# Feed-forward product order and later modulation copies in a one-core inference step

## The chip, the cores and the metric

The kernel runs on one core of a Trainium2 chip. The metric is the device time of one execution in microseconds, and three runs of the kernel before gave 1444.48, 1445.78 and 1446.87. TensorE (PE) multiplies, VectorE (DVE) and ScalarE (ACT) work on tiles, GpSimd (POOL) does some subtractions, and SyncE (SP) only issues DMAs; POOL and ACT can issue DMAs too. Every engine works through its own instructions in a fixed order, and semaphores make it wait for the others.

## The reference, cut to what matters

The reference is one layer of a backbone with two mixers for 128 context tokens and 512 latent tokens, in float32. The six modulation vectors come from a product with the large weight `ada_w`, the projection `w_in` has 10 x 1024 columns, and the feed-forward is a gated one with 2816 hidden columns:

```python
mod = (jax.nn.silu(cond) @ p['ada_w'] + p['ada_b']).reshape(cond.shape[0], N_MOD, D_MODEL)
h = x * (1.0 + scale1) + shift1
proj = h @ p['w_in']
...
x = layer_norm(ALPHA * x + gate1 * mix, p['ln1_g'], p['ln1_b'])
h = x * (1.0 + scale2) + shift2
gt, up = jnp.split(h @ p['ffn_w_in'], 2, axis=-1)
ff = (jax.nn.silu(gt) * up) @ p['ffn_w_out']
x = layer_norm(ALPHA * x + gate2 * ff, p['ln2_g'], p['ln2_b'])
```

## The kernel before

Each float32 matrix is split into a high part (`...h`) and the rest (`...l`), and a product is three passes on PE: high by high, low by high, high by low. The high part of a weight is a cast on ACT (line 619, through the helper `split`), the low part a subtraction on DVE (line 181, the helper through which all two-operand operations go, POOL's too).

Two stages multiply by a scheme in the manner of Winograd: seven products of half size instead of eight make two half blocks for two half token sets. The class `Wino` holds it. M1 (114 to 329 us) has 14 blocks of `w_in`, numbered 0 to 13, and its tiles begin with `m`; the feed-forward (1000 to 1282 us) has 22 blocks of `ffn_w_in`, and its tiles begin with `f`. A block j needs two raw weight tiles of 512 KB, row 0 and row 1 (`rm0_j`, `rm1_j` in M1, `rf0_j`, `rf1_j` in the feed-forward), out of a pool of three buffers. From these come the split tiles `g` (from row 0 as it is, products 1 and 2), `a` (product 4), and, after four subtractions on the raw tiles in place, `s` (product 6), `u` (5 and 7) and `v` (3). `gate` (token g) does the first, `rest` (token w) the others. A raw buffer is free for the next load once its last split is done: row 1 after `u`, row 0 after `v`. SP issues the loads in order.

Products 1, 6, 7 and 4 add up in one PSUM bank `a` (`ma`, `fa`), 2 in bank `b`, 5 and 3 in bank `c`. Between them the running sum is copied out by ACT (`keep`, line 676): `c1` after 1, `u2` after 6, `u3` after 7, of which product 4 must wait for the last since it adds to the same bank. DVE then adds the other banks to these copies, and product 5 of a block must wait until the `c` bank of two blocks earlier has been read by the addition into `u2`. In the profile's rows `u2` and `u3` are both `mu` or `fu`.

What sets the order: M1 follows PLAN, a string of tokens: `61` is product 6 of block 1, `g3` and `w3` are the weights of block 3, `Q9` is the modulation's product of quarter 9, i.e. half n = i mod 2 of modulation block nb = i div 2. The feed-forward follows PERIOD, one tuple of tokens with block offsets that is repeated for each j. Both give the order in which the program is written; a scheduler then orders every engine's instructions, and so a token that moves can also move ACT's and DVE's work. The modulation in M1: `ada_next` loads a quarter's weights of 1 MB (`araw`, one buffer, line 397), a Q step multiplies it (`ada_quad`, line 406), and after each second quarter `ada_vec` has ACT copy the sum out of PSUM into `md` (line 417); for blocks 4 and 5 and 10 and 11 PE then sums it over groups (`adag`, line 420), for the others it transposes it (`adaT`, line 430), DVE adds the bias, and the results go to `modT` or, by SP, to memory. `SY` in the code is SP, `G` is POOL.

Of the kernel before, what the change touches and what calls it, by code (L numbers as in the profile page):

```python
# [115 lines left out]
    return {k: np.ascontiguousarray(v) for k, v in c.items()}  # L116


PLAN = """x0 k0 L0 k1 x4 k2 p mlp t L1 T0 x3 T4 A0 x2 D0 T2 A1 x1 L2 B0 M0 T1 D2 A2 M2 T3 h0 L3 B1 D1 A3 h1 B2 M1 D3 h2 h3 M3 h4 W2 W0 h5 h6 h7 W1 q V0 e0 B3 g0 W3 V1 m w0 e2 10 20 g1 50 11 60 g2 70 21 30 40 w1 w2 61 51 52 12 71 Q8 62 22 g3 w3 13 41 g4 53 72 Q9 42 31 63 w4 g5 23 14 w5 73 Q10 43 32 g6 w6 64 24 15 54 74 Q11 33 65 25 44 16 26 55 75 Q12 g7 34 w7 66 45 56 17 76 Q13 35 67 46 g8 27 57 w8 18 77 Q14 g9 g10 36 w9 28 19 68 37 29 58 78 Q15 69 47 59 w10 79 Q16 38 110 210 g11 610 49 111 510 39 48 w11 211 g12 611 112 w12 212 710 Q17 g13 511 711 Q18 410 113 w13 311 612 310 411 512 712 Q19 513 213 613 412 713 312 413 313"""
HMOD = "SVSSVSSS"  # L120
HSUB = "GVVVVGVG"
WSUB = "VGGVVGGG"
# [6 lines left out]
FFNP = "1-1 2-1 g1 w1"  # L129
FFNT = ("g2", "", "")  # L130
FFN0 = "51 61 12 22 w2 71"
PERIOD = (("g", 1), ("w", 1), ("6", 0), ("4", -1), ("1", 1), ("5", 0), ("7", 0), ("3", -1), ("2", 1))
WPRI = 2
HIE = """SSSSVVSVSVSSSSSSSVVVSVVSVSSVSSSSSSSSSSSSSSSSSSSSSSSSSSSSSSSSSSSSSSSSSSSSSSSSSSSSSSSSSSSSSSSSSSSSSSSSSSSSSSSSSS"""
LOOK = """22222012202102201120122111222222222222222222222222222222222222222222222222222222222222222222222222222222222222"""
# [27 lines left out]
def body(tc, I, O):  # L163
    nc = tc.nc
    V, S, G, PE, SY = nc.vector, nc.scalar, nc.gpsimd, nc.tensor, nc.sync
# [14 lines left out]
    def tt(out, a, b, op, eng=None):  # L180
        return (eng or V).tensor_tensor(out=out, in0=a, in1=b, op=op)  # L181
# [7 lines left out]
    def pool(name, bufs=1, space=None, side=None):  # L189
        kw = dict(name=name, bufs=bufs, reuse_waits="tile")  # L190
        if space is not None:
            kw["space"] = space
        if side is not None:
            kw["side"] = side
        cm = tc.tile_pool(**kw)
        p = cm.__enter__()
        return p, (lambda: cm.__exit__(None, None, None))
# [19 lines left out]
    def mm_bank(nm):  # L217
        return bank("mm", nm)
# [20 lines left out]
    w1 = sp.tile([EMB, ORD], F32, name="w1")  # L239
# [12 lines left out]
    w2 = sp.tile([P, ORD], F32, name="w2")  # L252
    w3 = sp.tile([P, 2, ORD], F32, name="w3")
# [122 lines left out]
    def run_unit(u):  # L376
        n = len(u.specs)
        pos = stream["pos"]
        advance(pos, n)
        ws = stream["hl"][pos:pos + n]  # L380
        stream["pos"] = pos + n
        u.fn(*ws)
# [12 lines left out]
    def ada_load(nb, i, q, tag, bufs, eng=SY):  # L395
        raw = q.tile([P, 4, 512], F32, tag=tag, bufs=bufs, name=f"araw{nb}_{i}")
        eng.dma_start(raw, ada_w.rearrange("(k p) n -> p k n", p=P)[:, 4 * i:4 * i + 4, nb * 512:nb * 512 + 512])
        ada["raw"][nb, i] = raw

    def ada_quad(nb, i):  # L400
        raw = ada["raw"].pop((nb, i))
        if i == 0:
            ada["ps"][nb] = mm_bank(f"ada{nb}")
        ps = ada["ps"][nb]
        for g in range(4):
            PE.matmul(ps[32 * g:32 * g + 32, :], scT[:, 4 * i + g, :], raw[:, g, :], start=i == 0, stop=i == 1)

    def ada_mods(nb, q):
        with tc.high_priority():
            for i in range(2):  # L410
                ada_quad(nb, i)
            ada_vec(nb, q)

    def ada_vec(nb, q):
        part, half = nb // 2, nb % 2
        md = q.tile([P, 512], F32, tag="md", bufs=1, name=f"md{nb}")
        S.copy(md, ada["ps"].pop(nb))
        if part in (2, 5):
            p2 = mm_bank(f"adag{nb}")
            PE.matmul(p2[0:2, :], cst[:, 128:130], md, start=True, stop=True)  # L420
            gr = q.tile([2, 512], F32, tag="md", bufs=1, name=f"gr{nb}")
            SY.dma_start(gr, I["ada_b"][:, nb * 512:nb * 512 + 512].to_broadcast([2, 512]))
            tt(gr, p2[0:2, :], gr, ALU.add)
            V.tensor_scalar(gr, gr, 1.0 / ALPHA, None, ALU.mult)
            SY.dma_start(gd[part // 3, :, half * 512:half * 512 + 512], gr)
            return
        slot = {0: 0, 1: 1, 3: 2, 4: 3}[part]
        p2 = mm_bank(f"adaT{nb}")
        for i in range(4):
            PE.transpose(p2[:, i * P:i * P + P], md[:, i * P:i * P + P], ident)  # L430
        v = p2.rearrange("p (k g r) -> p k g r", k=4, g=4)[:, :, :, 0:2]
        dst = modT[:, slot, half * 4:half * 4 + 4, :]
        b0 = 17 + slot * 8 + half * 4
        tt(dst, v[:, :, 0], prT2[:, b0:b0 + 4].unsqueeze(2).to_broadcast([P, 4, 2]), ALU.add)
        for g in range(1, 4):
            tt(dst, v[:, :, g], dst, ALU.add)
# [3 lines left out]
    vp, close_vp = pool("vp")  # L440
# [7 lines left out]
    def x_load(t):  # L448
        xs = se.tile([P, D], F32, tag="xs", bufs=3, name=f"xs{t}")
        SY.dma_start(xs, x_tok[t])  # L450
        return xs

    def x_transpose(t, xs):
        for q in range(2):
            ps = sc_bank(f"xT{t}_{q}")
            for k in range(4):
                PE.transpose(ps[:, k * P:k * P + P], xs[:, (4 * q + k) * P:(4 * q + k + 1) * P], ident)
            for i in range(2):
                cpy("x", 2 * t + q, xT.tiles[2 * q + i][:, :, t * P:t * P + P],
                    ps[:, i * 256:i * 256 + 256].rearrange("p (k t) -> p k t", k=2))  # L460
# [51 lines left out]
    def ktab(i):  # L512
        cs = slice(i * 768, i * 768 + 768)
        raw = wp.tile([P, 768], F32, tag="raw", bufs=RAW_BUFS, name=f"kt{i}")
        SY.dma_start(raw, I["kt"][:, cs])
        cpy("k", i, kth[:, cs], raw)
        tt(ktl[:, cs], raw, f32(kth[:, cs]), ALU.subtract, G if KSUB[i] == "G" else V)

    def kern_load(cc):
        c0 = cc * 256  # L520
        w4 = se.tile([P, 2, 256], F32, tag="w4", bufs=2, name=f"w4_{cc}")
        for hf in range(2):
            SY.dma_start(w4[hf * ORD:hf * ORD + ORD],
                         I["filt_w4"][0].rearrange("o (a n) -> o a n", a=2)[:, :, c0:c0 + 256])
        win = sp.tile([P, NB, 256], F32, tag="win", bufs=2, name=f"win{cc}")
        SY.dma_start(win, I["win"][:, :, c0:c0 + 256])
        return w4, win, skp_all[:, c0:c0 + 256]
# [68 lines left out]
    def kern_store(cc, out):  # L596
        for t, f, n in out:
            KQ.dma_start(kd[cc, :, f:f + n], t)
# [24 lines left out]
    class Wino:  # L623
# [70 lines left out]
        def period(self, j, n):  # L694
            return self.run(" ".join(f"{t}{j + d}" for t, d in PERIOD if 0 <= j + d < n))

# [25 lines left out]
    def start():  # L722
        stream["stop"] = 4
        xs, ld, ab = {}, {}, {}

        def step(op, i):
            if op == "x":
                xs[i] = x_load(i)
            elif op == "T":
                x_transpose(i, xs[i])  # L730
            elif op == "L":
                ld[i] = kern_load(i)
            elif op == "A":
                ab[i] = kern_a(i, ld[i])
            elif op == "B":
                ab[i] = kern_b(i, ab[i])
            elif op == "W":
                kern_store(i, ab[i])
            elif op == "k":
                ktab(i)  # L740
            elif op == "D":
                for n in range(2):
                    ada_load(i, n, se, "araw", 3)
            elif op == "Q":
                nb, n = divmod(i, 2)
                ada_quad(nb, n)
                if i < M1_ADA[1] * 2 - 1:
                    ada_next(i + 1)
                if n == 1:
                    ada_vec(nb, mo["y"])  # L750
            elif op == "M":
                ada_mods(i, se)
            elif op == "h":
                make_h(i)
            elif op == "V":
                run_unit(vu[i])
            elif op == "e":
                m1_operands(i)
            elif op == "m":
                m1_open()  # L760
            elif op in "gw1234567":
                m1.run(op + str(i))()
            else:
                dict(p=params_load, t=params_T, q=params)[op]()

        for tok in PLAN.split():
            if tok == "mlp":
                if HP:
                    with tc.high_priority():
                        filter_mlp()  # L770
                else:
                    filter_mlp()
                continue
            step(tok[0], int(tok[1:] or 0))


    M1 = []
# [4 lines left out]
    mo = {}  # L782
# [78 lines left out]
    m1 = Wino("m", lambda tag: mo["p"], m1_x, m1_cols, m1_done, M1PRI)  # L861

    def ada_next(i):
        ada_load(*divmod(i, 2), vp, "v", 1, G)

    def m1_open():
        close_sp()
# [917 lines left out]
```

## Time and profile before

| | us |
|---|---|
| median of three runs | 1445.78 |
| profiled execution | 1444.85 |
| its span, first to last instruction | 1442.4 |
| PE busy | 1382.4 (96%) |
| DVE busy | 998.9 (69%) |
| ACT busy | 617.4 (43%) |
| POOL busy | 72.6 (5%) |

The profile is one execution. A timeline row gives the start, the duration, the engine, the line, the operation with its tiles, and, in square brackets, how long the engine sat idle before it and what ended that. The busy share of PE is an average: it is full in the middle of the run and has gaps in M1 and in the feed-forward. Where the clock is given it is the mean granted TensorE clock of a stretch, 1.00 being the upper of its two levels, 2.4 GHz, and 0.50 the lower, 1.2 GHz.

### The profile page before, as it was taken

The page shows a single profiled execution, that of the slowest core. Times are in us where ns is not written, and L with a number is a line of the kernel's source. Part 1 is how long each engine was busy: PE and PEld are TensorE (multiplying, and loading weights), DVE is VectorE, ACT ScalarE, POOL GpSimd, SP SyncE. Part 2 cuts the span into 40 slices and gives each one's busy share as a digit, 9 for nine tenths or more (in the row PEclk, how much of TensorE's full clock was granted, in tenths as well). Part 3 has the DMA queues.
Part 4 walks back from the last instruction along what each step waited for, and adds up shares of the span by engine and source line. Part 5 has one row for each costly group of instructions (what it writes and reads, how often), then busy time and mean ns, then how long its engine had stood idle before and what let it go on. Part 6 is the DMA issues. An engine that isn't in the chain of part 4 may idle for free. (4 is left out here: it accounts for less than half of the span.)

```text
span 1442.4 us, 23457 instructions
## 1 busy us (share of the span) xinstructions
PE 1382.4 (96%) x9513; PEld 1297.4 (90%) x9513; DVE 998.9 (69%) x1751; ACT 617.4 (43%) x1011; POOL 72.6 (5%) x68
## 2 busy tenths in 40 slices
PE   5999999989999999999999999999999999999997
PEld 2698888889999998999999999988999999998886
DVE  6886775745888853638888786568977667756427
ACT  3654544432333211446665655227644344542111
POOL 4320000011000000000000000000000000000003
PEclk9999999999999999999999999999999999999999
DMA  7934665557333364432232223551343333257211
GB/s 245 327 136 139 210 194 156 169 183 251 96 92 92 107 211 146 144 119 83 63 102 61 76 57 113 180 182 73 109 123 104 108 115 106 88 177 278 83 59 73
DMA packets 195783, 195.63 MB, mean 136 GB/s; under 512 B 7581, under 2 KB 155773, under 8 KB 194908
## 3 DMA queue, kind: packets, MB, share of 16 engines
q1 hardware_dynamic: 188524, 167.17, 37.1%
q0 software_dynamic: 5424, 21.73, 4.3%
q10 hardware_dynamic: 1728, 5.24, 0.9%
q8 instruction: 74, 1.21, 0.3%
q14 instruction: 33, 0.27, 0.1%
HBM read 162.91 MB, written 31.21 MB: 135 GB/s over the span
## 5 line engine op out<-in xcount | busy, mean ns | idle before, releaser
L181 DVE TENSOR_TENSOR wl<-raw,wh 128x1024 fp32r<-128x1024 f32 x96 | 117.3, 1224 | 133.4 <-ACT wh L357 132.4
L357 ACT CAST wh<-raw 128x1024 fp32r<-128x1024 f32 x90 | 94.1, 1049 | 221.2 <-PE pb L611 41.0
L1423 PE MATMUL fo<-wh,act 128*128 128x512 f32 (+1 forms) x440 | 130.7, 380 | 0.0
L1423 PEld LDWEIGHTS fo<-wh,act 128*128 128x128 f32 x440 | 81.3, 188 | 15.9
L1423 PE MATMUL fo<-wl,act 128*128 128x512 f32 (+1 forms) x220 | 83.4, 379 | 0.0
L611 PE MATMUL hy<-hTh,wh 128*128 128x320 f32 x256 | 79.6, 311 | 0.0
L611 PE MATMUL hy<-hTh,wl 128*128 128x320 f32 x256 | 79.2, 309 | 0.0
L611 PE MATMUL hy<-hTl,wh 128*128 128x320 f32 x256 | 79.2, 309 | 0.0
L611 PE MATMUL f<-hTh,wh 128*128 128x320 f32 x224 | 70.8, 316 | 0.0
L611 PE MATMUL f<-hTl,wh 128*128 128x320 f32 x224 | 69.7, 311 | 0.0
L611 PE MATMUL f<-hTh,wl 128*128 128x320 f32 x224 | 69.3, 309 | 0.0
L181 POOL TENSOR_TENSOR y<-y,gb 128x512 f32<-128x512 f32 x8 | 11.6, 1454 | 900.8 <-ACT y L170 900.5
L1423 PEld LDWEIGHTS fo<-wl,act 128*128 128x128 f32 x220 | 41.4, 188 | 7.9
L611 PEld LDWEIGHTS hy<-hTh,wh 128*128 128x128 f32 x256 | 48.1, 188 | 0.0
L611 PEld LDWEIGHTS hy<-hTl,wh 128*128 128x128 f32 x256 | 48.1, 188 | 0.0
L611 PEld LDWEIGHTS hy<-hTh,wl 128*128 128x128 f32 x256 | 48.1, 188 | 0.0
L170 ACT ACT_TABLE_LOAD x36 | 46.2, 1283 | 1.4 <-PEq L1769 0.7
L707 PE MATMUL v<-wl,hTh 128*128 128x256 f32 x160 | 44.9, 285 | 1.6 <-DVE wl L181 1.6
L707 PE MATMUL v<-wh,hTl 128*128 128x256 f32 x160 | 45.1, 285 | 0.2 <-POOL hTl L181 0.2
L707 PE MATMUL v<-wh,hTh 128*128 128x256 f32 x160 | 44.8, 285 | 0.0
L611 PEld LDWEIGHTS f<-hTl,wh 128*128 128x128 f32 x224 | 42.2, 188 | 0.0
L611 PEld LDWEIGHTS f<-hTh,wh 128*128 128x128 f32 x224 | 42.2, 188 | 0.0
(2291 smaller groups left out, 4730.9 us busy)
## 6 DMA issues: line engine op xcount, KB each, us to landing
raw<-in_w_in SPq DMA_DIRECT2D x52, 512.0 KB, 3.8
rf<-in_ffn_w_in SPq DMA_DIRECT2D x42, 512.0 KB, 4.0
araw<-in_ada_w POOLq DMA_DIRECT2D x16, 1024.0 KB, 5.7
rm<-in_w_in SPq DMA_DIRECT2D x28, 512.0 KB, 3.8
raw<-in_ffn_w_out SPq DMA_DIRECT2D x22, 512.0 KB, 3.7
sd<-my SPq DMA_DIRECT2D x28, 320.0 KB, 3.6
araw<-in_ada_w SPq DMA_DIRECT2D x8, 1024.0 KB, 11.3
kk<-kd SPq DMA_DIRECT2D x20, 256.0 KB, 3.1
```

Of the source, the lines that this page charges most:

```text
L170: r = S.activation(out, in_, func, bias=bias, scale=scale)
L181: return (eng or V).tensor_tensor(out=out, in0=a, in1=b, op=op)
L357: (V.tensor_copy if HIE[i] == "V" else S.copy)(hi, raw)
L611: r = PE.matmul(ps[:, 0:HT], w[a][:, k, :], x[b][:, k, c0:c0 + HT], start=k == 0 and i == 0, stop=k == kt - 1 and i == 2)
L707: PE.matmul(ps[:, (t - t0) * 256:(t - t0) * 256 + 256], hT[b][:, k, t * P:t * P + P], w[a][:, k % 4, :], start=k == 0 and i == 0, stop=k = ...
L1423: PE.matmul(ps, x(t, b, k0 + kk), w[a][:, kk, :], start=first and kk == 0 and i == 0, stop=last and kk == nk - 1 and i == 2)
```

## The change

Three things change. In PERIOD product 1 of the next block stands ahead of product 4 of the last. In PLAN `ada_vec` is no longer done by the second Q step of a modulation block but by tokens of its own, Z4 to Z9, each set some nine steps later: Z4 stands ahead of Q10 where the copy was part of Q9, Z5 behind Q12 where it was part of Q11, and the last, Z9, at the very end of PLAN. And `ada_next` no longer passes `G`, so the twelve `araw` loads of M1 are issued by SP.

```diff
-PERIOD = (("g", 1), ("w", 1), ("6", 0), ("4", -1), ("1", 1), ("5", 0), ("7", 0), ("3", -1), ("2", 1))
+PERIOD = (("g", 1), ("w", 1), ("6", 0), ("1", 1), ("4", -1), ("5", 0), ("7", 0), ("3", -1), ("2", 1))
...
                 if i < M1_ADA[1] * 2 - 1:
                     ada_next(i + 1)
-                if n == 1:
-                    ada_vec(nb, mo["y"])
+            elif op == "Z":
+                ada_vec(i, mo["y"])
...
     def ada_next(i):
-        ada_load(*divmod(i, 2), vp, "v", 1, G)
+        ada_load(*divmod(i, 2), vp, "v", 1)
```

In the feed-forward this is DVE's row around the weights of blocks 13 and 14, before (a name is the tile, its block and a number; `wfg14l` is the low part of the `g` tile of block 14):

```order
L181 TENSOR_TENSOR wfg14l_12101<-rf0_14_12098,wfg14h_12100 128x1024
L181 TENSOR_TENSOR rf1_13_11973<-rf0_13_11967,rf1_13_11973 128x512
L181 TENSOR_TENSOR rf0_13_11967<-rf1_13_11973,rf0_13_11967 128x512
L181 TENSOR_TENSOR rf0_13_11967<-rf0_13_11967 128x512
L181 TENSOR_TENSOR wfs13l_11983<-rf0_13_11967,wfs13h_11982 128x512
L181 TENSOR_TENSOR wfu13l_11987<-rf1_13_11973,wfu13h_11986 128x1024
L181 TENSOR_TENSOR fu3_11_11931<-fc11_11906,fu3_11_11931 128x320
L181 TENSOR_TENSOR wfv13l_11992<-rf0_13_11967,wfv13h_11991 128x512
L181 TENSOR_TENSOR fu2_10_11745<-fc10_11775,fu2_10_11745 128x320
```

And the same row in the changed kernel:

```order
L181 TENSOR_TENSOR wfg14l_12101<-rf0_14_12098,wfg14h_12100 128x1024
L181 TENSOR_TENSOR wfa13l_11976<-rf1_13_11973,wfa13h_11975 128x512
L181 TENSOR_TENSOR y10_11702<-fa10_11616,y10_11702 128x320
L181 TENSOR_TENSOR rf1_13_11973<-rf1_13_11973 128x512
L181 TENSOR_TENSOR rf1_13_11973<-rf0_13_11967,rf1_13_11973 128x512
L181 TENSOR_TENSOR rf0_13_11967<-rf1_13_11973,rf0_13_11967 128x512
L181 TENSOR_TENSOR rf0_13_11967<-rf0_13_11967 128x512
L181 TENSOR_TENSOR wfu13l_11987<-rf1_13_11973,wfu13h_11986 128x1024
L181 TENSOR_TENSOR wfs13l_11983<-rf0_13_11967,wfs13h_11982 128x512
L181 TENSOR_TENSOR wfv13l_11992<-rf0_13_11967,wfv13h_11991 128x512
L181 TENSOR_TENSOR fu3_11_11931<-fc11_11906,fu3_11_11931 128x320
L181 TENSOR_TENSOR fu2_10_11745<-fc10_11775,fu2_10_11745 128x320
```

The split `wfa13l` and the first subtraction on `rf1_13` stood ahead of `wfg14l` and now stand behind it, with a `y` product between them; `wfs` and `wfu` change places, and both `fu` additions come after `wfv13l`. ACT's casts move in the same way.

At M1's start this is ACT's row before:

```order
L619 CAST wmg2h_1442<-rm0_2_1440 128x1024
L676 COPY mc1_1_1424<-ma1_1411 128x320
L619 CAST wma1h_1510<-rm1_1_1508 128x512
L676 COPY mu2_0_1438<-ma0_1361 128x320
L619 CAST wmu1h_1521<-rm1_1_1508 128x1024
L676 COPY mu3_0_1458<-ma0_1361 128x320
```

And in the changed kernel:

```order
L619 CAST wmg2h_1442<-rm0_2_1440 128x1024
L676 COPY mc1_1_1424<-ma1_1411 128x320
L676 COPY mu2_0_1438<-ma0_1361 128x320
L676 COPY mu3_0_1458<-ma0_1361 128x320
L619 CAST wma1h_1510<-rm1_1_1508 128x512
```

Both copies of block 0's sums now stand ahead of the cast `wma1h`, which needs a loaded tile.

On SP, in the changed kernel, the loads around blocks 10 to 12 of M1 stand like this (`araw7_1` is the second quarter of modulation block 7, `sd` stores a finished half block):

```order
L397 DMA araw7_1_2475<-in_ada_w 128x4x512
L633 DMA rm1_10_2683<-in_w_in 128x8x128
L633 DMA rm0_11_2786<-in_w_in 128x8x128
L845 DMA sd_137<-my0_6_2151 128x640
L845 DMA sd_137<-my0_7_2389 128x640
L397 DMA araw8_0_2640<-in_ada_w 128x4x512
L845 DMA sd_137<-my1_7_2456 128x640
L397 DMA araw8_1_2727<-in_ada_w 128x4x512
L633 DMA rm1_11_2886<-in_w_in 128x8x128
```

The three `araw` rows stood on POOL before; the other rows of SP keep their order there.

## Rows read from the trace of the kernel before

**Rows 1.** The page's head: the span and the busy time of the engines.

```profile
span 1442.4 us, 23457 instructions
...
PE 1382.4 (96%) x9513; PEld 1297.4 (90%) x9513; DVE 998.9 (69%) x1751; ACT 617.4 (43%) x1011; POOL 72.6 (5%) x68
```

**Rows 2.** Stretches of the span: their length, then the busy time of each engine with its number of instructions, the granted clock, the DMA share and GB/s.

```profile
950.00:1000.00 50.00, 50.00 (x254) 42.40 (x253) 39.53 (x89) 24.33 (x44) 0.00 (x0) 1.00 0.29 95
...
1084.87:1227.96 143.09, 136.10 (x913) 133.38 (x912) 100.08 (x163) 61.12 (x109) 0.00 (x0) 1.00 0.36 107
```

**Rows 3.** What PE waited for from 100 to 360 us: total in us, times, the longest; the row on a weight tile.

```profile
PE ma L668 <- DVE wms11l L181: 0.5, 1, 0.5
```

**Rows 4.** The timeline of PE: the single instructions of M1 ahead of which it waited over 1 us.

```profile
127.71 0.41 PE L668 MATMUL ma<-m7h,wmu0h 128*128 128x320 f32 x1 [3.18 <-ACT mu L676]
...
165.27 0.42 PE L668 MATMUL mc<-m5h,wmu3h 128*128 128x320 f32 x1 [1.73 <-DVE mu L181]
...
190.09 0.59 PE L420 MATMUL adag<-md,cst 128*2 128x512 f32 x1 [1.05 <-ACT md L417]
...
220.26 0.33 PE L430 MATMUL adaT<-cst,md 128*128 128x128 f32 x1 [1.92 <-ACT md L417]
...
288.11 0.33 PE L430 MATMUL adaT<-cst,md 128*128 128x128 f32 x1 [1.64 <-ACT md L417]
...
307.01 0.63 PE L668 MATMUL mc<-m5h,wmu12h 128*128 128x320 f32 x1 [4.00 <-DVE mu L181]
```

**Rows 5.** The timeline of ACT from 126 us.

```profile
126.71 0.62 ACT L619 CAST wma1h<-rm 128x512 fp32r<-128x512 f32 x1 [3.14 <-DMA rm<-in_w_in]
127.24 0.42 ACT L676 COPY mu<-ma 128x320 f32<-128x320 f32 x1
```

**Rows 6.** The timelines of DVE and of POOL around 302 us, with an earlier row of DVE of the same form.

```profile
287.69 1.22 DVE L181 TENSOR_TENSOR wmu12l<-rm,wmu12h 128x1024 fp32r<-128x1024 f32 x1
...
302.58 3.37 DVE L181 TENSOR_TENSOR wmu13l<-rm,wmu13h 128x1024 fp32r<-128x1024 f32 x1
...
302.15 2.72 POOL L181 TENSOR_TENSOR wl<-raw,wh 128x1024 fp32r<-128x1024 f32 x1 [7.50 <-DVE wh L357]
```

**Rows 7.** Stretches that begin where a wait of PE ended, of PE alone: length, busy time with its number of instructions, granted clock, DMA share, GB/s.

```profile
127.71:134.00 6.29, 6.29 (x32) 0.73 0.01 3
220.26:226.00 5.74, 5.74 (x30) 0.70 1.00 324
307.01:315.00 7.99, 7.99 (x35) 0.61 0.91 290
1141.64:1144.00 2.36, 2.36 (x16) 1.00 0.08 22
...
288.11:292.00 3.89, 3.89 (x28) 1.00 0.98 338
```

**Rows 8.** Two lines of the page on DMA issues (KB each, median us from issue to landing), and the timelines of POOL, SP and ACT around 260 us.

```profile
araw<-in_ada_w POOLq DMA_DIRECT2D x16, 1024.0 KB, 5.7
rm<-in_w_in SPq DMA_DIRECT2D x28, 512.0 KB, 3.8
...
259.00 0.75 POOL L397 DMA_DIRECT2D araw<-in_ada_w  x1 [7.92 <-PE ada L406]
...
259.47 1.59 SPq L633 DMA_DIRECT2D rm<-in_w_in  x2
...
268.31 1.05 ACT L619 CAST wmg12h<-rm 128x1024 fp32r<-128x1024 f32 x1 [5.39 <-DMA rm<-in_w_in]
```

**Rows 9.** What PE waited for from 995 to 1285 us, and two rows of its timeline: the start of product 5 of block 12, and a wait ahead of product 4.

```profile
PE fa L668 <- ACT fu L676: 8.5, 12, 1.3
...
1155.28 0.42 PE L668 MATMUL fa<-t4h,wfa11h 128*128 128x320 f32 x1 [1.08 <-ACT fu L676]
...
1158.90 0.31 PE L668 MATMUL fc<-xxh,wfu12h 128*128 128x320 f32 x1
```

**Rows 10.** The chain that ended last, in order of time, its longest pieces: start, us, what.

```profile
1157.19 6.20 DMA rf<-in_ffn_w_in
1170.94 5.20 DMA rf<-in_ffn_w_in
...
1237.36 1.76 PE fc L668 x12
```

**Rows 11.** The timeline of ACT, two turns of the feed-forward's loop.

```profile
1149.66 1.05 ACT L619 CAST wfg14h<-rf 128x1024 fp32r<-128x1024 f32 x1 [2.41 <-DMA rf<-in_ffn_w_in]
...
1163.41 1.05 ACT L619 CAST wfg15h<-rf 128x1024 fp32r<-128x1024 f32 x1 [2.44 <-DMA rf<-in_ffn_w_in]
```

**Rows 12.** The timeline of DVE in the same turn.

```profile
1150.75 1.23 DVE L181 TENSOR_TENSOR wfg14l<-rf,wfg14h 128x1024 fp32r<-128x1024 f32 x1 [2.04 <-ACT wfg14h L619]
...
1154.94 1.23 DVE L181 TENSOR_TENSOR wfu13l<-rf,wfu13h 128x1024 fp32r<-128x1024 f32 x1 [0.25 <-ACT wfu13h L619]
...
1156.48 0.68 DVE L181 TENSOR_TENSOR wfv13l<-rf,wfv13h 128x512 fp32r<-128x512 f32 x1
...
1161.00 0.69 DVE L181 TENSOR_TENSOR wfa14l<-rf,wfa14h 128x512 fp32r<-128x512 f32 x1 [1.94 <-ACT wfa14h L619]
1161.73 0.69 DVE L181 TENSOR_TENSOR rf<-rf 128x512 f32<-128x512 f32 x1
```

**Rows 13.** The timeline of SP.

```profile
1156.19 1.75 SPq L633 DMA_DIRECT2D rf<-in_ffn_w_in  x2
```

More of the change, by code (lines that the diff above doesn't have):

```diff
@@ L116, in _constants @@
     return {k: np.ascontiguousarray(v) for k, v in c.items()}
-PLAN = """x0 k0 L0 k1 x4 k2 p mlp t L1 T0 x3 T4 A0 x2 D0 T2 A1 x1 L2 B0 M0 T1 D2 A2 M2 T3 h0 L3 B1 D1 A3 h1 B2 M1 D3 h2 h3 M3 h4 W2 W0 h5 h6 h7 W1 q V0 e0 B3 g0 W3 V1 m w0 e2 10 20 g1 50 11 60 g2 70 21 30 40 w1 w2 61 51 52 12 71 Q8 62 22 g3 w3 13 41 g4 53 72 Q9 42 31 63 w4 g5 23 14 w5 73 Q10 43 32 g6 w6 64 24 15 54 74 Q11 33 65 25 44 16 26 55 75 Q12 g7 34 w7 66 45 56 17 76 Q13 35 67 46 g8 27 57 w8 18 77 Q14 g9 g10 36 w9 28 19 68 37 29 58 78 Q15 69 47 59 w10 79 Q16 38 110 210 g11 610 49 111 510 39 48 w11 211 g12 611 112 w12 212 710 Q17 g13 511 711 Q18 410 113 w13 311 612 310 411 512 712 Q19 513 213 613 412 713 312 413 313"""
+PLAN = """x0 k0 L0 k1 x4 k2 p mlp t L1 T0 x3 T4 A0 x2 D0 T2 A1 x1 L2 B0 M0 T1 D2 A2 M2 T3 h0 L3 B1 D1 A3 h1 B2 M1 D3 h2 h3 M3 h4 W2 W0 h5 h6 h7 W1 q V0 e0 B3 g0 W3 V1 m w0 e2 10 20 g1 50 11 60 g2 70 21 30 40 w1 w2 61 51 52 12 71 Q8 62 22 g3 w3 13 41 g4 53 72 Q9 42 31 63 w4 g5 23 14 w5 73 Z4 Q10 43 32 g6 w6 64 24 15 54 74 Q11 33 65 25 44 16 26 55 75 Q12 Z5 g7 34 w7 66 45 56 17 76 Q13 35 67 46 g8 27 57 w8 18 77 Z6 Q14 g9 g10 36 w9 28 19 68 37 29 58 78 Q15 69 47 59 w10 79 Q16 38 110 210 Z7 g11 610 49 111 510 39 48 w11 211 g12 611 112 w12 212 710 Q17 g13 511 711 Q18 410 113 w13 311 612 Z8 310 411 512 712 Q19 513 213 613 412 713 312 413 313 Z9"""
 HMOD = "SVSSVSSS"
```

## The prediction

> **What bounds the kernel now.** I read the page's head first: TensorE (PE) is busy 1382.4 of 1442.4 us [rows 1], so only about 60 us of idle time and any time at a low clock can be won. Then I read PE's waits by stage. In the middle, from 350 to 1000 us, PE is nearly full (50.00 us busy in 950 to 1000 [rows 2]), and whatever the first Winograd stage ("M1", 114 to 329 us) wins or loses passes through it to the end. Two stages wait. In M1 PE waits for single copies on ScalarE (ACT) and subtractions on VectorE (DVE) [rows 4]. In the feed-forward it waits 8.5 us in all, 12 times, at most 1.3, for ACT's copy `fu` of the seventh product, always ahead of the fourth product [rows 9].
>
> What paces the feed-forward is another matter. The chain that ended last has no PE in its long pieces from 1003 to 1233 us: it goes from one `rf` weight load to the next [rows 10], and PE is busy 136.10 of 143.09 us [rows 2]. The loop in one block, with t = 0 at the gate cast `wfg14h` at 1149.66: DVE's `wfg14l` at 1.09, the raw-tile subtractions at 2.23 and 3.68, `wfu13l` at 5.28 to 6.51, `wfv13l` until 7.50 [rows 12]; the two issues of the next `rf` loads begin at 1156.19, t = 6.53 [rows 13]; the second of them, 6.20 us in the chain from 1157.19 [rows 10], ends the idle time of ACT and lets `wfg15h` start at 1163.41 [rows 11]. That is 13.75 us a turn, against PE's seven products of 1.76 us [rows 10], 12.3. So the stream of weights is the pace, and PE's wait for `fu` is how it is held to that pace: the copy stands in ACT's row behind the casts of a later block.
>
> **The change, part by part.** *Modulation copies (tokens Z).* Each `md` copy and what PE does with it moves some nine steps later; the copy then has many products of cover. PE's waits for `md` go: 1.05 + 1.92 + 1.64 = 4.61 us [rows 4]. The same transposes, additions and stores are issued later, none is saved or added.
>
> *What the scheduler reorders in M1.* The 3.18 us at 127.71 come from ACT: the copy `mu` (0.42 us at 127.24) stood behind `wma1h`, which waited 3.14 us for a DMA [rows 5]. In the changed order both `mu` copies stand ahead of `wma1h`, so PE's product 7(0) no longer waits; the cover is the products up to 5(1), which needs `wmu1l`, and by these rows that comes perhaps 0.4 us late. The 4.00 us at 307.01 come from DVE: `wmu13l` took 3.37 us, while `wmu12l` of the same form took 1.22, and GpSimd (POOL) ran `wl` from 302.15 to 304.87 [rows 6]. `mu` of block 11, for which PE waited, stood behind it. Now `wmu13l` and that `mu` stand ahead of the cast that starts POOL's `wl`, so this wait goes too. What is beside POOL's `wl` then is `wmv13l`, with `mu` of block 10 behind it, which PE's 5(13) needs: between 0 and 2.15 (3.37 - 1.22), I take 1.0, since PE comes there two products later.
>
> The GPSIMD Engine Reference of the Trainium skill (1. Specifications) says that GpSimd shares its way into SBUF with VectorE and that DVE instructions with two SBUF inputs contend with it. The long `wmu13l` agrees; by that rule `wmv13l` is stretched and the 1.0 would rather be 2.15, by a private port it would be 0.
>
> *The clock.* After three of these waits the granted clock was low for a while, means of 0.73, 0.70 and 0.61 over the 6.29, 5.74 and 7.99 us behind them, where 1.00 is the upper and 0.50 the lower of its two levels [rows 7]. Lost is (1 - clock) x length: 1.70 + 1.72 + 3.12 = 6.54 us, and this goes with the waits. After the wait of 1.64 at 288.11 and after one in the feed-forward it stayed at 1.00 [rows 7].
>
> *`araw` loads on SP's queue.* Twelve loads of 1 MB leave POOL's queue and stand in SP's, in order; ten of them directly or nearly ahead of a weight load `rm`. Each waits for PE to be done with the `araw` before it, and what stands behind it waits too. The trace of before has no such queue in M1. Lower bound 0: in before the same bytes share the same engines (5.7 us from POOL's queue, 3.8 for an `rm` [rows 8]). Upper bound: an `rm` lands half an `araw` later, 2.85 us, wherever PE has no slack. Such a place is near 277 us, where PE already waits for `wms11l` [rows 3] and ACT waited 5.39 us for the `rm` of `wmg12h` [rows 8]; three loads stand close to it (`araw7_1`, `araw8_1`, `araw9_0`): 8.6 us. The ends are far apart; the rows at 277 say "no slack", those at 259 that the `araw` was issued on POOL within half a microsecond of the `rm` pair anyway [rows 8]. I take the middle, 4.3.
>
> The Trainium skill's DMA: Bandwidth & Descriptors (Issuing engines are not separate DMA queues) says that transfers started by different engines run on the same 16 DMA engines and interleave, and that a second issuer saves only issue time. By that rule the term is 0 and not 4.3; it leaves out the wait that an `araw` brings into SP's row, which no row of before shows.
>
> Sum for M1: -4.61 - 3.18 - 4.00 - 6.54 + 0.4 + 1.0 + 4.3 = -12.6 us (ends: -18.3 with none of the three additions, -7.2 with 0.4, 2.15 and 8.6).
>
> *The feed-forward's order.* In time t of the loop, with the durations of [rows 12]: the changed order leaves the `wfa` split and the first subtraction on `rf1` no longer in DVE's idle time ahead of `wfg` (in before at 1161.00 and 1161.73, with 2.41 to 2.44 us of idle time of ACT around them [rows 11, 12]) but sets them behind `wfg14l`, together with a `y` product. So: `wfg14l` 1.09 to 2.23, `wfa13l` to 2.83, `y` to 3.23, then four dependent subtractions at 0.72 each (0.69 plus the gap to the next, 1161.73 against 1161.00) to 6.0, `wfu13l` 6.0 to 7.25, `wfs13l` and `wfv13l` to 8.5. In before `wfu13l` ended at 6.51 and `wfv13l` at 7.50. The first buffer comes free 0.7 later, the second 1.0. The loads take what they took, so a turn takes between 0.7 and 1.0 us longer; I take 0.8. The stream sets the pace from `wfg9` to `wfg20`, 1084.87 to 1227.96, eleven turns at 13.0: 11 x 0.8 = 8.8. PE cannot give this back: it goes on only when `fu` is copied (t about 6.6 now, 5.6 in before), and product 5 now waits for DVE's `fu` behind `wfv13l` at t about 9.3 (9.24 in before, 1158.90 [rows 9]). So PE's one wait of 1.1 a block becomes two of about 1.0, neither as long as those after which the clock fell [rows 4, 7]. Product 1 as cover for product 4, 1.76 us, is worth nothing to a loop in which PE is not.
>
> Sum: 1444.85 for the profiled execution, -12.6 + 8.8 = -3.8, 1441.05; its span is 1442.4 and 2.4 lie outside. The median of the runs is 0.9 above it, so 1442.
>
> **The rivals.** *A, PE's wait is what paces the feed-forward.* Then product 1 ahead of 4 covers 1.3 us of 1.76 each time and the 8.5 us go: 1445.8 - 12.6 - 8.5 = 1425. For it: PE does wait there, and by no other releaser. Against: the chain of [rows 10] and ACT's idle time, which ends with the DMA, not with PE.
>
> *B, the feed-forward is the same.* The 0.8 is hidden because the two loads share the engines and the later first issue only makes them overlap more: 1445.8 - 12.6 = 1433. For it: the second load took 5.20 us in some turns and 6.20 in others [rows 10]; against: each turn's load begins as soon as its buffer is free.
>
> *C, slower: `araw` in front of `rm` on SP.* With 2.85 us at each of six of the ten such places M1 pays 17.1 instead of 4.3 and wins almost nothing: 1442 + 12.8 = 1455. It decides from three places: 8.6 in place of 4.3 makes M1 -8.3, and with the feed-forward's 8.8 the sum is +0.5. For it: each load waits for PE's quad and holds what stands behind; against: mostly the `rm` behind has its own wait on DVE that ends later.
>
> *D, the copies' waits only move:* PE meets the next late thing at each place, and M1 wins but 4.6: 1445.8 - 4.6 + 8.8 = 1450. For it: 5(3) waited 1.73 for DVE with no `md` near [rows 4].
>
> **How the numbers follow.** Forecast 0.48 at 1442, by its own bounds (M1 -18.3 to -7.2, the feed-forward 11 x 0.7 to 11 x 1.0) 1435 to 1450; A 0.12; B 0.16; C 0.12; D 0.12. Faster by over 0.2% (below 1442.9, about what a measurement of this kernel can tell from no change): A and B, 0.28, and 0.27 of the forecast: 0.55. Slower (above 1448.7): C, most of D and little of the forecast: 0.24. The same: 0.21. The range leaves out A and the far end of C: 1428 to 1454.
>
> **What would show it.** Right: in the feed-forward turns of `wfg` of about 14.3 us instead of 13.7, a wait of PE at product 4 and a second at product 5 for DVE's `fu`, `wfa` casts right behind `wfg`; in M1 no wait of PE for `md` nor at 7(0), and a clock of 1.00 at 128 to 134 and 220 to 226. Wrong: turns of 13.7 or less, or PE at 12.3 a block; a wait of PE for `wms` or `wmu` above 3 us in M1, with SP's `araw` issued just ahead of the `rm` it waits for.

## The result, and the profile after

The changed kernel takes 1433.8 us (median of 4 runs, 1432.18 to 1434.42) against 1445.63 of the kernel before: 11.8 us less, a ratio of 0.9916 with a 95% interval of 0.9899 to 0.9933. The forecast was 1442, the range 1428 to 1454. The profiled execution has a span of 1431.9 us.

Both halves of the sum came with the forecast sign: the first stage won, the feed-forward lost. From the first product of M1 to the first `hy` product, from there to the first `fb` product, and from there to the first `fo` product, PE's timeline gives:

| us | M1 | the middle | feed-forward |
|---|---|---|---|
| before | 214.8 | 672.6 | 280.4 |
| after | 193.2 | 672.7 | 288.5 |
| difference | -21.6 | +0.1 | +8.1 |
| forecast | -12.6 | 0 | +8.8 |

The profiled execution came to M1 2.4 us later than that of before, with more lost at a low clock ahead of it; over all the profiles below this start lies between 113.8 and 116.6 us with nothing changed ahead of it, so the stages are compared by their own lengths.

The head of the page after, and three stretches of M1 (PE alone: length, busy time with its number of instructions, granted clock, DMA share, GB/s):

```profile
span 1431.9 us, 23453 instructions
...
PE 1381.0 (96%) x9513; PEld 1293.4 (90%) x9513; DVE 992.3 (69%) x1751; ACT 617.3 (43%) x1011; POOL 64.1 (4%) x56
```

```profile
123.00:134.00 11.00, 11.00 (x74) 1.00 0.54 172
210.00:216.00 6.00, 6.00 (x46) 1.00 0.69 217
288.00:296.00 8.00, 8.00 (x56) 1.00 0.84 245
```

PE is busy without a gap where it waited 3.18, 1.92 and 4.00 us before [rows 4], and the clock stays at 1.00 where it had been 0.73, 0.70 and 0.61 [rows 7]. What PE still waited for from 100 to 360 us (total, times, longest):

```profile
PE mc L668 <- DVE wmu0l L181: 0.3, 1, 0.3
PE ma L668 <- ACT mu L676: 0.2, 1, 0.2
PE mc L668 <- DVE mu L181: 0.2, 1, 0.2
PE ada L406 <- DMA araw<-in_ada_w: 0.2, 1, 0.2
```

That is all: the `md` waits are gone, and so are those that the prediction had left standing. The queue that it feared shows once, with 0.2 us.

At M1's start ACT now goes like this:

```profile
124.76 1.05 ACT L619 CAST wmg2h<-rm 128x1024 fp32r<-128x1024 f32 x1 [1.81 <-DMA rm<-in_w_in]
125.71 0.42 ACT L676 COPY mc<-ma 128x320 f32<-128x320 f32 x1
126.17 0.43 ACT L676 COPY mu<-ma 128x320 f32<-128x320 f32 x1
128.72 0.43 ACT L676 COPY mu<-ma 128x320 f32<-128x320 f32 x1 [2.12 <-PE ma L668]
129.22 0.62 ACT L619 CAST wma1h<-rm 128x512 fp32r<-128x512 f32 x1
```

Before, the copy stood behind a cast that waited for a DMA [rows 5]. Now ACT waits for PE, not PE for ACT. PE's own row changed here too, which the section on the change does not show and the prediction did not look at: product 3 of block 0, for one, ran between two halves of product 4 before, and now runs ahead of all of it.

Near the end of M1, DVE and POOL:

```profile
287.71 1.22 DVE L181 TENSOR_TENSOR wmu13l<-rm,wmu13h 128x1024 fp32r<-128x1024 f32 x1
...
291.20 0.69 DVE L357 CAST wh<-raw 128x1024 fp32r<-128x1024 f32 x1 [0.59 <-DMA raw<-in_w_in]
291.81 0.68 DVE L181 TENSOR_TENSOR wmv13l<-rm,wmv13h 128x512 fp32r<-128x512 f32 x1
...
292.02 2.72 POOL L181 TENSOR_TENSOR wl<-raw,wh 128x1024 fp32r<-128x1024 f32 x1 [202.39 <-DVE wh L357]
```

`wmu13l` takes 1.22 us instead of 3.37 [rows 6], since POOL's `wl` begins after it. And `wmv13l` beside that `wl` takes 0.68, no more than elsewhere: it had begun 0.2 us ahead of POOL.

In the feed-forward, one turn of the loop on DVE, with ACT's g cast at either end of it:

```profile
1132.46 1.05 ACT L619 CAST wfg14h<-rf 128x1024 fp32r<-128x1024 f32 x1 [3.06 <-DMA rf<-in_ffn_w_in]
...
1146.11 1.05 ACT L619 CAST wfg15h<-rf 128x1024 fp32r<-128x1024 f32 x1 [2.86 <-DMA rf<-in_ffn_w_in]
```

```profile
1133.55 1.23 DVE L181 TENSOR_TENSOR wfg14l<-rf,wfg14h 128x1024 fp32r<-128x1024 f32 x1 [4.59 <-ACT wfg14h L619]
1134.69 0.69 DVE L181 TENSOR_TENSOR wfa13l<-rf,wfa13h 128x512 fp32r<-128x512 f32 x1
1135.29 0.49 DVE L181 TENSOR_TENSOR y<-fa,y 128x320 f32<-128x320 f32 x1
1135.69 0.69 DVE L181 TENSOR_TENSOR rf<-rf 128x512 f32<-128x512 f32 x1
...
1138.47 1.22 DVE L181 TENSOR_TENSOR wfu13l<-rf,wfu13h 128x1024 fp32r<-128x1024 f32 x1
...
1140.21 0.68 DVE L181 TENSOR_TENSOR wfv13l<-rf,wfv13h 128x512 fp32r<-128x512 f32 x1
```

With t = 0 at 1132.46, `wfu13l` starts at 6.01 and `wfv13l` ends at 8.43 (forecast 6.0 and 8.5; 5.28 and 7.50 before [rows 12]). PE's waits from 985 to 1280 us, and the two kinds in this turn:

```profile
PE fc L668 <- DVE fu L181: 8.6, 14, 0.9
PE fa L668 <- ACT fu L676: 4.0, 10, 1.0
...
1139.13 0.41 PE L668 MATMUL fa<-t4h,wfa11h 128*128 128x320 f32 x1 [0.39 <-ACT fu L676]
...
1141.75 0.42 PE L668 MATMUL fc<-xxh,wfu12h 128*128 128x320 f32 x1 [0.59 <-DVE fu L181]
```

The one wait per block for ACT's `fu`, 8.5 us in all [rows 9], has become two: product 4 begins at t = 6.67 and product 5 at 9.29 (forecast 6.6 and 9.3). The twelve turns from `wfg9` to `wfg21` take 163.1 us instead of 156.1. In these turns the chain that ended last still goes from one `rf` load to the next, with one stretch through PE between 1141.75 and 1150.8:

```profile
1127.09 5.35 DMA rf<-in_ffn_w_in
1141.75 2.03 PE fc L668 x12
...
1154.56 5.26 DMA rf<-in_ffn_w_in
```

A part of the 8.1 us was made by no edit. Early in the feed-forward PE waits 2.15 us for ACT's `b12h`, in the kernel before as in the changed one. Behind this wait the granted clock stayed at 1.00 before; after, its mean was 0.83 over 10 us, so some 1.7 us were lost (PE's timeline, then the stretches, before ahead of after):

```profile
1006.64 0.41 PE L1572 MATMUL fg<-b12h,wh 128*128 128x320 f32 x1 [2.15 <-ACT b12h L619]
987.52 0.41 PE L1572 MATMUL fg<-b12h,wh 128*128 128x320 f32 x1 [2.15 <-ACT b12h L619]
...
1006.64:1016.64 10.00, 10.00 (x67) 1.00 0.38 104
987.52:997.52 10.00, 10.00 (x58) 0.83 0.38 104
```

### The profile page after: what moved, and what is told of

It reads as the page before. It is cut to its first block, busy times and chain, and to the rows that moved or that the text cites. A ratio compares the mean times of both kernels' runs of the same rounds, so it can differ in the third digit from the quotient of the medians.

```text
span 1431.9 us, 23453 instructions
## 1 busy us (share of the span) xinstructions
PE 1381.0 (96%) x9513; PEld 1293.4 (90%) x9513; DVE 992.3 (69%) x1751; ACT 617.3 (43%) x1011; POOL 64.1 (4%) x56
```

## The experiments

Each kernel was timed beside the kernel before. M1 and feed-forward are the lengths defined above, from one profile each. In round brackets behind them stands what was lost in the stage at a low clock in that profile, (1 - granted clock) x length; the 6.8 of the kernel before are the prediction's 6.5 with 0.3 that fell into a wait.

| kernel | time, us | ratio (95% interval) | M1 | feed-forward |
|---|---|---|---|---|
| kernel before | 1445.6 | | 214.8 (6.8) | 280.4 (0) |
| changed kernel | 1433.8 | 0.9916 (0.9899 to 0.9933) | 193.2 (0) | 288.5 (1.7) |
| m1only | 1427.0 | 0.9862 (0.9841 to 0.9883) | 193.4 (0) | 281.3 (1.7) |
| period | 1452.3 | 1.0037 (1.0024 to 1.0051) | 212.3 (3.4) | 289.6 (0) |
| z_only | 1439.4 | 0.9950 (0.9933 to 0.9967) | 209.3 (3.4) | 282.0 (1.7) |
| sp_only | 1428.2 | 0.9872 (0.9846 to 0.9897) | 196.6 (0) | 281.4 (1.7) |
| after_order | 1417.3 | 0.9813 (0.9796 to 0.9830) | 194.5 (0) | 272.7 (0) |
| after_4raw | 1423.6 | 0.9855 (0.9834 to 0.9875) | 194.8 (0) | 278.0 (3.4) |
| m1_4raw | 1423.9 | 0.9859 (0.9841 to 0.9878) | 193.9 (0) | 279.6 (3.4) |
| copy_first | 1438.6 | 0.9956 (0.9938 to 0.9974) | 209.0 (5.1) | 279.7 (0) |
| cast_first | 1431.0 | 0.9904 (0.9878 to 0.9930) | 197.6 (0) | 282.8 (1.7) |
| order_4raw | 1420.1 | 0.9832 (0.9801 to 0.9862) | 194.7 (0) | 275.3 (3.4) |

The lost clock differs between profiles of one and the same order. In period the rows of PE, ACT, DVE and POOL in M1 stand in the order of before, every instruction of them, and yet M1 is 2.5 us shorter, with 3.4 us less lost. A difference of this size between two single profiles is not an edit's.

**The three parts one by one.** m1only is the changed kernel with the old order of products:

```diff
-PERIOD = (("g", 1), ("w", 1), ("6", 0), ("1", 1), ("4", -1), ("5", 0), ("7", 0), ("3", -1), ("2", 1))
+PERIOD = (("g", 1), ("w", 1), ("6", 0), ("4", -1), ("1", 1), ("5", 0), ("7", 0), ("3", -1), ("2", 1))
```

> The changed kernel with the feed-forward's old order (product 4 of the last block ahead of product 1 of the next). Theory 1 (the new order costs the feed-forward 8 us, 1271.07 - 982.57 against 1282.10 - 1001.69): the feed-forward takes 280.4 us as before, fb to fo, and the time is 1433.8 - 8.1 = about 1425.7. Rival (the feed-forward got longer because it starts earlier or because the first stage's other changes reach into it): the feed-forward stays at 288.5 and the time at 1433.8.

Measured 1427.0, the feed-forward at 281.3. The loss belongs to the edit of PERIOD.

period is the kernel before with the opposite edit alone.

> The kernel before with the feed-forward's new order alone. Its rows of VectorE and ScalarE in the feed-forward stand as before (the a split and the first raw subtraction ahead of the next g split), unlike in the changed kernel. Theory 1 (the loss is in VectorE's row, not in TensorE's): the feed-forward takes 280.4 us or less, up to 8 less if product 1 covers the wait ahead of product 4, time 1438 to 1446. Theory 2 (the loss comes from TensorE's order, product 5 right behind product 4): the feed-forward takes 288.5 and the time is 1445.6 + 8.1 = 1453.7.

Measured 1452.3, the feed-forward at 289.6. The expectation rests on a wrong premise: in the kernel that ran, VectorE's and ScalarE's rows stand as in the changed kernel, `wfa` behind the next `wfg`, not as before. So the run shows that this part alone costs what the changed kernel loses, but it doesn't tell the two theories apart. With the clock alike the cost is 7.2 us between m1only and the changed kernel and 9.2 between the kernel before and this one.

z_only has the Z tokens in PLAN, as in the changed kernel, with `araw` on POOL's queue and the old product order:

```diff
-                if n == 1:
-                    ada_vec(nb, mo["y"])
+            elif op == "Z":
+                ada_vec(i, mo["y"])
```

> The kernel before with the Z tokens alone (later modulation copies; araw loads on POOL's queue, old product order). ScalarE's row at 127 us and VectorE's at 302 us stand nearly as before. Theory: only the waits for md go, 4.61 us, and 1.72 us of low clock behind the one at 220.26: 1445.6 - 6.3 = 1439.3. Rival (the waits move to the next late thing): 1443 or more. Rival (Z makes the whole gain of the first stage): 1426.5.

Measured 1439.4, the expected number, in part by luck. No `md` is among the waits of M1, but the waits for `mu` are larger than before, so that PE's idle time in M1 fell by only 1.8 us (14.9 to 13.1) and the lost clock by 3.4:

```profile
PE mc L668 <- DVE mu L181: 6.2, 2, 5.2
PE ma L668 <- ACT mu L676: 6.0, 2, 3.2
```

The 5.2 is the wait at 5(12) again, behind a subtraction that POOL lengthens: here it is `wmv13l`, with 2.83 us instead of the 0.68 that it took in the changed kernel.

```profile
299.52 2.83 DVE L181 TENSOR_TENSOR wmv13l<-rm,wmv13h 128x512 fp32r<-128x512 f32 x1
...
299.09 2.71 POOL L181 TENSOR_TENSOR wl<-raw,wh 128x1024 fp32r<-128x1024 f32 x1 [9.81 <-DVE wh L357]
```

sp_only moves the loads to SP's queue and nothing else:

```diff
-        ada_load(*divmod(i, 2), vp, "v", 1, G)
+        ada_load(*divmod(i, 2), vp, "v", 1)
```

> The kernel before with the araw loads on SP's queue alone. With this the copies at 127 us stand ahead of the cast wma1h, and wmu13l and mu of block 11 ahead of POOL's wl. Theory: the queue itself costs nothing and the scheduler's other order takes away the waits at 127.71 and 307.01 with their low clock, 3.18 + 1.70 + 4.00 + 3.12 = 12.0, the md waits stay: 1445.6 - 12 = 1433.6. Rival (a load in SP's row holds the weight loads behind it, hidden in the changed kernel by the Z tokens): 1440 or more, with waits of TensorE for wms or wmu.

Measured 1428.2, M1 at 196.6: 18.2 us less, the largest part of the gain, though the edit moves no computation. What PE waited for there:

```profile
PE adaT L430 <- ACT md L417: 2.0, 1, 2.0
PE mc L668 <- DVE mu L181: 0.4, 1, 0.4
PE ma L668 <- ACT mu L676: 0.4, 1, 0.4
```

No wait for a weight tile of over 0.3 us, so the loads in SP's row hold nothing up. Nor do loads land faster: from 105 to 330 us the median from issue to landing is 5.7 us for `araw` from either queue, and for `rm` 6.4 instead of 5.9. With the queue the scheduler chose another order on ACT and DVE (the copies ahead of `wma1h`, `wmu13l` and `mu` of block 11 ahead of POOL's `wl`) and on PE, where product 3 of block 0 began at 126.88, ahead of product 4, instead of at 133.45 between two halves of it:

```profile
133.45 0.31 PE L668 MATMUL mc<-hTh,wmv0h 128*128 128x320 f32 x1
...
126.88 0.41 PE L668 MATMUL mc<-hTh,wmv0h 128*128 128x320 f32 x1
```

Only one `md` wait is left of three. Z and SP apart win 5.5 and 18.2 us of M1, together, in the changed kernel, 21.6.

**Queue or order?** copy_first keeps POOL's queue and the old plan and makes two edits of order: ACT's cast `wma1h` is put behind the copies of block 0 with a manual dependency, and the subtraction `wl` of raw tile 5 goes to DVE.

```diff
-WSUB = "VGGVVGGG"
+WSUB = "VGGVVVGG"
...
+            if (self.nm, nm, j) == ("m", "a", 1):
+                order_after(c, self.copied)
```

> The kernel before with two edits in the first stage and the araw loads on POOL's queue: ScalarE's copies of block 0 forced ahead of the cast wma1h, and the subtraction wl5, POOL's, given to VectorE. Theory (the gain of the queue move lies in the order that the scheduler then chose): the wait at 127.71 goes with its low clock, 4.9 us less by 150 us, less about 0.4; wmu13l takes 1.22 instead of 3.37 us, and the wait ahead of 5(12) stays in part, as wl5 now takes its own 1.14 us of VectorE there. Time 1440 to 1436. Rival (the queue itself delays the weight loads): TensorE then waits as long for wms or wmu of block 1 and the time stays at 1445.

Measured 1438.6. The wait at 127 us is gone with the old queue, and `wmu13l` takes 1.22:

```profile
300.09 1.22 DVE L181 TENSOR_TENSOR wl<-raw,wh 128x1024 fp32r<-128x1024 f32 x1
301.22 1.22 DVE L181 TENSOR_TENSOR wmu13l<-rm,wmu13h 128x1024 fp32r<-128x1024 f32 x1
```

So the wait at 127 us goes by the order alone, without the queue; PE's products in this place then stand as in sp_only. M1 is 5.8 us shorter: PE's idle time fell by 4.3 us (14.9 to 10.6), what the shorter `wmu13l` gives being in it, and the lost clock by 1.7. A wait of 3.23 us at 5(12) stays, with no POOL beside it. That the other 12 us of sp_only come from the order too fits its waits and its loads, but no run shows it. cast_first tries the opposite, the copy behind the cast with the queue on SP; for that the token w1 moves in PLAN from ahead of w2 to directly behind g1:

```diff
+            if (self.nm, nm, j) == ("m", "u2", 0):
+                order_after(c, self.cast)
```

> m1only (the changed kernel with the old product order) with ScalarE's copy of block 0 forced behind the cast wma1h again; the araw loads stay on SP's queue. Theory (the gain at 127 us came from the order in ScalarE's row, not from the queue): TensorE waits for mu ahead of 7(0) some 3 us, the clock falls behind it, and the time is 1427.0 + 4.9 = 1432. Rival (the queue made it): no wait there, 1427.

Measured 1431.0, the expected size, but not by the expected way. To write the cast first its token had to move, and then its load came first too: `wma1h` ran at 123.37, the copy at 124.70 hardly waited, and PE had no wait at 7(0). The 4.2 us of M1 come from other waits, the longest 1.6 for DVE's `mu`. The run doesn't decide the question.

**The loop of the feed-forward.** after_order is the changed kernel, TensorE's order included, with one order forced: the `a` split of a block and the first subtraction on its raw tile stand ahead of the next block's `g` split on ACT and DVE.

```diff
                     W[j, 1] = W[j, 2] = self.split("g", j, W[j, 0], wp, "w", HL_BUFS)
+                    if self.nm == "f" and j - 1 in self.hold:
+                        for x, y in zip(self.sp, self.hold[j - 1]):
+                            order_after(x, y)
...
-                tt(u[:, 4:8], u[:, 0:4], u[:, 4:8], ALU.add)
+                self.hold[j] = self.sp[0], tt(u[:, 4:8], u[:, 0:4], u[:, 4:8], ALU.add)
```

> The changed kernel with one order forced in the feed-forward: on ScalarE and VectorE the a split of a block and the first subtraction on its raw tile stand ahead of the next block's g split again, as in the kernel before; TensorE's order stays the new one. Theory 1 (the new place of the a split lengthens the loop of the weight stream): a turn of wfg is back at 13.0 us on the mean from block 9 to 21 (13.59 in the changed kernel), the feed-forward at 280.4 us instead of 288.5, the time at about 1426. Theory 2 (TensorE's order, product 5 right behind 4, waiting for VectorE's fu): the feed-forward stays at 288.5 and the time at 1433.8.

Measured 1417.3, the fastest of all, 16.5 us below the changed kernel and 1.9% below the kernel before. The feed-forward takes 272.7 us. PE's row in it is instruction for instruction that of the changed kernel; ACT's and DVE's alone moved. PE's waits from 975 to 1285 us, the chain there (start, us, what), and DVE's and ACT's rows:

```profile
PE fc L671 <- DVE fu L181: 2.4, 5, 1.2
PE fg L1575 <- ACT b12h L619: 2.2, 1, 2.2
```

```profile
1096.30 2.03 PE fc L671 x12
1098.33 1.77 PE fa L671 x12
...
1133.75 5.71 DMA rf<-in_ffn_w_in
```

```profile
1139.48 1.05 ACT L619 CAST wfg15h<-rf 128x1024 fp32r<-128x1024 f32 x1 [2.03 <-DMA rf<-in_ffn_w_in]
1140.43 0.42 ACT L679 COPY fu<-fa 128x320 f32<-128x320 f32 x1
...
1144.03 1.22 DVE L181 TENSOR_TENSOR wfu14l<-rf,wfu14h 128x1024 fp32r<-128x1024 f32 x1
```

`wfu14l` now ends at t = 5.77 (6.51 before, 7.23 changed), twelve turns take 149.6 us, and the copy `fu` stands directly behind the `g` cast, at t = 0.95 instead of 6.2: PE has no wait for ACT's `fu` left, and product 1 does cover product 4. The chain has stretches of PE in it again. So the loss lay in the casts and subtractions that the scheduler moved with PERIOD, not in PE's order: of the 15.8 us between the two kernels the clock has 1.7. The rows are not those of the kernel before again (`wfu` stands ahead of `wfs`, the `fu` copy forward), so the 7.7 us beyond the forecast can't be given to one of them.

after_4raw and m1_4raw give the feed-forward a fourth raw buffer, with the new and the old product order:

```diff
+            if self.nm == "f" and j % 2 == 1 and row == 0:
+                t = self.p("raw").tile([P, KT, P], F32, tag="raw4", bufs=1, name=f"r{self.nm}{row}_{j}")
+            else:
+                t = wp.tile([P, KT, P], F32, tag="raw", bufs=RAW_BUFS, name=f"r{self.nm}{row}_{j}")
```

> The changed kernel with a fourth raw buffer in the feed-forward, taken by row 0 of the odd blocks (a small constant tile shares another's place to make room). Theory (the loop runs from the release of a raw buffer through its load to the next cast): with four buffers a load has the time of two blocks, TensorE sets the pace with 7 x 1.757 = 12.3 us plus small waits, the twelve turns from wfg9 to wfg21 take about 150 us instead of 163.1, and the time is 1433.8 - 13 = about 1421. Rival (TensorE's waits for fu pace the feed-forward whatever the loads do): turns of 13.6 and 1433.8.

> The same fourth raw buffer with the feed-forward's old product order, the first stage as changed. Theory: the loop of the weights is no longer the pace, and the waits of TensorE for fu, 8.3 us in m1only, become small: 1427.0 - 8 = 1419. Rival: those waits are TensorE's own and stay: 1427.

Measured 1423.6 and 1423.9. The new order then loses nothing against the old (278.0 and 279.6), and twelve turns of after_4raw take 153.8 us: the raw buffers were the pace. The rest of the expected gain went to the start: a wait of 3.4 instead of 2.2 for `b12h` and others for `t2h` and `xh`, with 3.4 us of lost clock instead of 1.7. The fourth buffer also changes the order of the rows there, PE's among them, so these two runs change more than the buffers. order_4raw puts it on top of after_order.

> after_order (the changed kernel with the a split forced ahead of the next g split) and a fourth raw buffer in the feed-forward besides. Theory: TensorE already runs at 12.5 us a block in after_order against 12.3 of products, and waits 2.4 us in all; a fourth buffer can win at most that, 1417.3 - 2 = 1415. Rival (TensorE waits elsewhere for the loads of the first blocks, as it did in after_4raw): 1420 or more.

Measured 1420.1, the rival: PE has no wait for `fu` at all, but pays at the start as the other two do (3.4 for `b12h`). In the feed-forward it loses 3.4 us at a low clock where after_order loses none; without that it would be at 271.9 against 272.7.

## Why the prediction was right, and where it was off

The sign was right, and the time lay in the range, but -3.8 was forecast and -11.8 came. 1433 stands in the prediction as rival B's number, for a reason that did not hold: the feed-forward did not stay the same.

*The feed-forward* went by the working: the chain of loads as the pace, the `a` split and a `y` product behind `wfg`, `wfu` ending at 7.25 (7.23 measured), product 4 at 6.6 (6.67) and 5 at 9.3 (9.29). +8.1 against +8.8. That these two are so near is in part luck. The eleven turns from `wfg9` to `wfg20`, for which 8.8 was worked out, took 149.6 us instead of 143.1: 6.5, or 0.6 a turn where 0.8 was taken. The other 1.6 lies outside them, and 1.7 of the stage is the lost clock behind `b12h`, which the prediction did not have. By its own sign, "turns of 13.7 or less", the prediction would have been wrong: the mean turn was 13.6. The sign was set wrongly, by the one turn of 13.75, while its sum starts from the mean of before, 13.0.

Two sizes were off. The turn shown took 13.65 us where 14.3 was expected: the second load took 5.2 from the end of `wfv13l` instead of the 6.20 of rows 10, as it had in some later turns of before already (5.20). So the turns from `wfg10` to `wfg15` got 0.3 longer and those to `wfg21` 0.9. And PE's two waits were about 0.4 and 0.6, not 1.0 each. Rival A, that PE's own wait is the pace, is refuted: with the cover of product 1 the stage got longer, and with the cast order forced under the same product order it fell by 15.8.

*M1* was the right mechanism with a wrong sum. The terms taken away were right: with the low clock 18.3 us, by the rows. But three additions of 0.4, 1.0 and 4.3 measured next to nothing, and three waits that no step touched, 1.73, 0.68 and 0.47, went too: 18.3 + 2.9 = 21.2, less 0.6 by which the smallest waits grew, 20.6 against 21.6 measured; the last 1.0 is not accounted for. The 6.5 of low clock in the 18.3 belong to the one profile that the prediction read: in period, with the same order, waits of 3.30 at 7(0) and 2.03 for `md` had a clock of 1.00 behind them.

The step that failed most is the one on "`araw` loads on SP's queue". It took the middle between 0 and 8.6, on the ground that PE had no slack at 277 us. The lower bound was right: the `araw` loads cost 0.2 us, as the rule in the Trainium skill's DMA: Bandwidth & Descriptors (Issuing engines are not separate DMA queues) had it, and the wait that they bring into SP's row held up nothing. The slack argument failed: where it saw none, PE no longer waits for `wms11l`, and ACT's wait for the `rm` of `wmg12h` fell from 5.39 us [rows 8] to 1.34:

```profile
257.44 1.05 ACT L619 CAST wmg12h<-rm 128x1024 fp32r<-128x1024 f32 x1 [1.34 <-DMA rm<-in_w_in]
```

Perhaps the weight stream of M1 moves forward with PE, since the three buffers of `a` tie `wma` of a block to PE's product 4 of an earlier one; no run shows that. Moreover this part was read as a cost and was the larger gain: the prediction credited the reordered rows to the scheduler without asking which edit made them, and sp_only shows that it was the queue's.

*5(13) behind `wmv13l`*, taken as 1.0 and by the rule in the Trainium skill's GPSIMD Engine Reference (1. Specifications) rather as 2.15, cost nothing, since `wmv13l` started 0.2 us ahead of POOL. z_only shows the other case, 2.83 us or 2.15 more than usual, where POOL started 0.4 us ahead. So DVE and POOL did contend, as that rule has it; which of the two began first decided here.

Rival C, weight loads held on SP, and D, waits that move on, are refuted for the changed kernel; z_only shows D in part (its waits for `mu` grew from 9.6 to 12.2 us).

## What to carry to other kernels

Before giving a wait of the busiest engine a price, find the loop that sets the pace of the stage: here the cover for PE's wait made the stage 8 us longer with the scheduler's order of casts, and 8 us shorter than at first once the `a` split was held ahead of the next `g` split. A change of issuing queue can move the order of PE, ACT and DVE far from the load, so ask of each reordered row which edit made it, by building the parts alone. A wait may be followed by a low clock, 6.5 of the 18.3 us in M1, but it need not be: the same wait in the same order had one behind it in some profiles and none in others, so take the lost clock out before two single profiles are compared.

## What was not expected of the hardware

A DVE subtraction with two SBUF operands beside POOL's of 2.7 us took 3.37 instead of 1.22 and 2.83 instead of 0.68 when POOL had begun first, and its usual 0.68 when it had begun first itself. The two long ones ended 1.08 and 0.55 us behind POOL's end, as if held until it was done.

The length of a wait of PE did not tell whether a low clock would follow. In the kernel before 1.92, 3.18 and 4.00 us were followed by a granted clock of 0.50 and 1.64 was not; in period 2.03 and 3.30 were not, nor was 2.02 in sp_only, and in copy_first one of 1.30 behind another of 0.97 was. The wait of 2.15 us for `b12h` stands in nine of the twelve profiles: five have a granted clock of 0.50 soon behind it (the changed kernel, m1only, z_only, sp_only, cast_first), four stay at 1.00 (the kernel before, period, after_order, copy_first). Period's two stretches behind 3.30 and 2.03:

```profile
128.90:135.19 6.29, 6.29 (x42) 1.00 0.01 3
219.86:225.60 5.74, 5.74 (x40) 1.00 1.05 342
```

Why the same pair of `rf` loads takes about 6 us in some turns and 5.2 in others stays open: most of the early turns of the kernel before have the one, most of its late turns and of the changed kernel's the other (one of 6.10 and one of 5.98 apart), and no run was made for it.
